# HGRN2 blocks half a period behind the RWKV blocks, and head totals as two fp32r passes over a split operand

## The chip, the cores and the metric

The kernel runs on one core of one Trainium2 chip. The metric is the device time of one execution in microseconds: 2369.66 us, the median of three runs (2367.89 to 2370.66).

## The reference, cut to what matters

Two layers work on a sequence of 2048 tokens with 1024 features. Layer 0 projects its modulated input to nine streams of 512 columns, and mixes them in two ways. The HGRN2 half has 4 heads of 128 columns; the RWKV half has 8 heads of 64 columns. Layer 1 is a gated linear recurrence (RG-LRU). Each layer ends with an output projection, a residual and a layer norm. What is computed in the places that the change touches:

```python
# HGRN2, per head of 128: chunked decayed attention, then
o = o * lax.rsqrt(jnp.mean(o * o, -1, keepdims=True) + RMS_EPS)
# RWKV-7, per head of 64:
kk = heads(k * k_k)
kk = kk * lax.rsqrt(jnp.maximum(jnp.sum(kk * kk, -1, keepdims=True), 1e-24))
y = rwkv7_scan(rh, heads(decay), kh, vh, -kk, kk * icl)
y_var = jnp.mean(jnp.square(y - y_mu), -1, keepdims=True)
y = y + jnp.sum(rh * kh * r_k.astype(f32), -1, keepdims=True) * vh
```

The three totals over a head of 64 (of `kk*kk`, of `rh*kh*r_k`, of the squared centred `y`) are the totals that the change rewrites.

## The kernel before

The tokens go through in two superblocks of 1024 (`sb`), each of two halves of 512 (`b`). For every layer and superblock there are a preparation of the input (`make_h`, `prep_h`), a mixer (`mix0`, `mix1`) and an output stage (`out_proj`). Every large projection is three passes of fp32r matmuls over operands split into a high and a low part (`mm3`, L430 to L433; `split`, L366).

The order of TensorE in `mix0` (L1227 to L1284) is written by hand. `projections()` yields once per step, and one step is two of the eight `k` of a projection, so six matmuls of 128x512. 16 steps are the low-rank projection, then 48 steps per group `g` (three RWKV and three HGRN2 projections of two halves), and 64 steps are the gates. The other work is a list of tasks, each with the step at which it starts; a task goes on until its next `yield n` and comes back `n` steps later. The other engines are ordered by a list scheduler in which earlier written instructions have precedence, and `tc.high_priority(offset=n)` moves an instruction up by `n`.

For a group `g` and a half `b` an RWKV block (`b_steps`, L844) starts at step 40+48g+24b, and the HGRN2 block of the same `g`, `b` (`a_steps`, L630) at 64+48g+24b, which is the step at which the next RWKV block starts. The period is thus 24 steps. With the start of the block as step 0, TensorE does in an RWKV block: `pss` (total for `kk`) at 2, `psc` at 8 and 10, `pbn` and `pv` at 12, `pk` at 14, `pzt` and `pg` at 16, then the 16x16 triangular inverse on VectorE (L969 to L974, 15 pairs of a multiply and a reduce), which goes out to DRAM and comes back as `xd` (L977 to L982) and is transposed to `xn` (L984); `plq` at 22 reads `xn`; `pzq` at 24, four ScalarE copies into `x32` (L1008), the transpose `xm` (L1010, named `xn` in the code), `plx` at 26, `pz` 28, `pwv` 30, `pmq` 32, the eight states one step apart from 34 (`pn`, each followed by L1090 on VectorE), `py` at 42 and `pvr` (total for the variance) at 44. In an HGRN2 block: the decays of levels 5 and 0 at 0, `scores` of these and the decays of levels 1 and 2 at 4, `scores` of these, the decays of 3 and 4 and the exponentials at 8, the last `scores` at 14, `pk` at 16, `pst` at 18, `po` at 20, `pss` at 22. The total in that block (L785, L786) is already two fp32r passes over a split operand.

The three totals of an RWKV block are one fp32 matmul each with the block matrix `bones` (L864, L925, L1112). There are 16 RWKV blocks in the run.

The gates (`gate_steps`, L570) follow from step 208; at step 256 the output weights are fetched (`fetch`, L474) into tiles whose tags are listed in `WO0` (L60), four of which are tags of the HGRN2 block, and `half` (L487) splits them at 264 and 272. Projection results, inputs and gates live in tiles of the pool `up` (L101), 11 of them.

Of the kernel before, what the change touches and what calls it, by code (L numbers as in the profile page):

```python
# [13 lines left out]
F32 = mybir.dt.float32  # L14
F32R = mybir.dt.float32r
BF16 = mybir.dt.bfloat16
U8 = mybir.dt.uint8
AF = mybir.ActivationFunctionType
ALU = mybir.AluOpType
# [4 lines left out]
P = 128  # L24
# [7 lines left out]
INV_STEPS = 6  # L32
# [23 lines left out]
for _n, _w in VEC_FIELDS:  # L56
# [1 line left out]
    _o += _w  # L58
NVEC = _o
WO0 = (  # L60
    (1, "b_kk", 1), (1, "b_m1", 1), (1, "b_ep", 1), (3, "b_bk", 1), (1, "a_b", 1), (1, "a_e", 1), (1, "a_lf", 1),
    (1, "a_kz", 1), (2, "b_zg", 1), (2, "b_bkt", 1), (2, "b_sv", 2),
)

DBG = {}
# [3 lines left out]
def tile_encoder(  # L69
# [19 lines left out]
    nc = tc.nc  # L89
# [8 lines left out]
    cst = ctx.enter_context(tc.tile_pool(name="cst", bufs=1))  # L98
    hp = ctx.enter_context(tc.tile_pool(name="hp", bufs=1))
    wp = ctx.enter_context(tc.tile_pool(name="wp", bufs=4))  # L100
    up = ctx.enter_context(tc.tile_pool(name="up", bufs=11))  # L101
    sp_ = ctx.enter_context(tc.tile_pool(name="sp", bufs=1))
    pool = [None]

# [12 lines left out]
    tp = _Cur()  # L117
# [13 lines left out]
    make_identity(nc, ident)  # L131
    ones = cst.tile([P, 1], F32, name="ones")
    nc.vector.memset(ones, 1.0)
    bones = cst.tile([P, P], F32, name="bones")
    nc.vector.memset(bones, 1.0)
    ones_r = cst.tile([P, P], F32R, name="ones_r")
    nc.vector.tensor_copy(ones_r, bones)
    nc.vector.memset(bones[0:64, 64:128], 0.0)
    nc.vector.memset(bones[64:128, 0:64], 0.0)

    cen = cst.tile([P, P], F32, name="cen")
    nc.vector.scalar_tensor_tensor(out=cen, in0=bones, scalar=-1.0 / 64.0, in1=ident, op0=ALU.mult, op1=ALU.add)
# [6 lines left out]
    def V(name, i):  # L149
        o = VOFF[name] + i  # L150
        return vec[:, o : o + 1]
# [214 lines left out]
    def split(hi, lo, src, eng=None, hi_eng=None):  # L366
        (hi_eng or nc.scalar.copy)(hi, src)  # L367
        return (eng or nc.vector).tensor_tensor(out=lo, in0=src, in1=hi.bitcast(F32), op=ALU.subtract)  # L368
# [434 lines left out]
    xd = cst.tile([P, 8, 32], F32, name="xd")  # L803
    nc.gpsimd.memset(xd, 0.0)

    def rate_steps(p, sb, b, lr, sgi_of):

        sgi = sgi_of[p, b] = tp.tile([P, 2, BLK], F32, name=f"sgi_{p}_{sb}_{b}", tag="sgi")
        w2a2_sb = tp.tile([P, P], F32, name=f"w2a2_{p}_{sb}_{b}", tag="w2a2")
        nc.sync.dma_start(w2a2_sb, w2a2[:, p * P : (p + 1) * P])  # L810
        yield 2
        ls = slice(b * BLK, (b + 1) * BLK)

        pws = [ps.tile([P, BLK], F32, name=f"pw_{p}_{sb}_{i}_{b}", tag="tb", bufs=2) for i in range(2)]
        for i in range(2):
            rows = slice(64 * i, 64 * i + 64)
            nc.tensor.matmul(pws[i], w2a2_sb[rows], lr[rows, ls], start=True, stop=True)
        for i, bias in enumerate(("w0", "a0")):
            last = nc.scalar.activation(sgi[:, i], pws[i], AF.Sigmoid, bias=V(bias, p))
        ln_exp_after(last)  # L820
# [23 lines left out]
    def b_steps(p, sb, b, us, sgi_of):  # L844
# [3 lines left out]
        nm = f"b{p}_{sb}_{b}"  # L848
# [9 lines left out]
        ep = tp.tile([P, 8, 65], F32, name=f"ep_{nm}", tag="b_ep")  # L858
        sq = ep.rearrange("p c t -> p (c t)")[:, 0:BLK]
        nc.scalar.activation(sq, k, AF.Square, scale=V("kk", p))  # L860
        nc.scalar.activation(kkr, k, AF.Identity, scale=V("kk", p))
        yield 2
        pss = ps.tile([P, BLK], F32, name=f"pss_{nm}", tag="tb", bufs=2)
        nc.tensor.matmul(pss, bones, sq, start=True, stop=True)  # L864
        m = t2k("b_m1")
        mx = nc.vector.tensor_scalar_max(m, pss, 1e-24)
        exact_ln(m, m, mx, scale=131072.0)
# [24 lines left out]
        nc.vector.tensor_mul(bk[:, :, 1], v64(icl), v64(em))  # L892

        nc.vector.scalar_tensor_tensor(out=icl, in0=r, scalar=V("rk", p), in1=icl, op0=ALU.mult, op1=ALU.mult)

        sc = tp.tile([P, 2, 8, P], F32, name=f"zb_{nm}", tag="b_sc", bufs=2)
        msk = bmask.rearrange("p (o c) -> p o c", o=1).broadcast_to([P, 4, P])
# [24 lines left out]

        yield 2
        pbn = ps.tile([P, BLK], F32, name=f"pbn_{nm}", tag="tb", bufs=2)
        nc.tensor.matmul(pbn, bones, icl, start=True, stop=True)  # L925

# [37 lines left out]
        nc.gpsimd.memset(xt, 0.0)  # L966
        for q in range(2):
            nc.gpsimd.memset(xt.rearrange("p n i -> p (n i)")[64 * q : 64 * q + 64, q:128:18], 1.0)
        for i in range(1, 16):  # L969
            n = i // 2 + 1  # L970
            pv_ = pr[:, 0 : n * (i + 1)].rearrange("p (n j) -> p n j", j=i + 1)
            av = ai[:, 0 : i + 1, i].rearrange("p (o j) -> p o j", o=1).broadcast_to([P, n, i + 1])
            nc.vector.tensor_mul(pv_, xt[:, 0:n, 0 : i + 1], av)
            nc.vector.tensor_reduce(out=xt[:, 0:n, i], in_=pv_, axis=AX.X, op=ALU.add)  # L974
        xd_dr = dram.tile([8, 8, 8, 2, 16], F32, name=f"xd_{nm}", tag="xd", bufs=2)
        for q in range(2):
            nc.sync.dma_start(xd_dr[:, :, :, q].rearrange("kb c n j -> (kb c) n j"), xt[64 * q : 64 * q + 64])  # L977
# [6 lines left out]
        nc.vector.transpose(xn, xd)  # L984
        x32 = tp.tile([P, 8, 32], F32, name=f"x32_{nm}", tag="b_ai")
        nc.gpsimd.tensor_copy(x32, xd)
        yield INV_STEPS

        plq = ps.tile([P, 8, 16], F32, name=f"plq_{nm}", tag="tb", bufs=2)
        for c in range(8):  # L990
# [16 lines left out]
        for hb in range(4):  # L1007
            nc.scalar.copy(x32[32 * hb : 32 * hb + 16, :, 16:32], pzq[32 * hb : 32 * hb + 16])  # L1008
        xn = tp.tile([P, 8, 32], F32, name=f"xm_{nm}", tag="b_xn")
        nc.vector.transpose(xn, x32)  # L1010
        tt = tt_tiles[tt_count[0] % 2]
        tt_count[0] += 1
        for hb in range(4):
            rs_ = slice(32 * hb, 32 * hb + 32)
            o_ = 32 * (hb % 2)
            nc.gpsimd.tensor_copy(tt[rs_, :, o_ : o_ + 32], x32[rs_])
        yield 2
        plx = ps.tile([P, 8, 32], F32, name=f"plx_{nm}", tag="tb", bufs=2)
        for c in range(8):
            for hd in range(2):  # L1020
# [50 lines left out]


        yield 2
        st = tp.tile([P, 7, 64], F32, name=f"sb_{nm}", tag="b_st")
        pn = ps.tile([P, 8, 64], F32, name=f"pn_{nm}", tag="cg")
        for c in range(8):
            for hd, hs in hds:
# [6 lines left out]
        for c in range(8):  # L1084
            if states[c] is not None:
                for hd, hs in hds:
                    nc.tensor.matmul(
                        pn[hs, c], sc[hs, 0, c, 0:64], states[c][hs], start=False, stop=True, skip_group_check=True
                    )
            nc.vector.tensor_scalar_mul(states[c + 1], pn[:, c], lam[:, c : c + 1])  # L1090
            yield 1
        py = ps.tile([P, 8, 64], F32, name=f"py_{nm}", tag="yb")
        for c in range(8):
# [13 lines left out]
        yp = py.rearrange("p c t -> p (c t)")  # L1107
        sq = zf[:, 0:BLK]
        nc.scalar.activation(sq, yp, AF.Square)
        yield 2  # L1110
        pvr = ps.tile([P, BLK], F32, name=f"pvr_{nm}", tag="cg")
        nc.tensor.matmul(pvr, bones, sq, start=True, stop=True)  # L1112
        rs = zf[:, BLK : 2 * BLK]
        nc.scalar.activation(rs, pvr, AF.Ln, scale=1.0 / 64.0, bias=eps_gn)
        nc.scalar.activation(rs, rs, AF.Exp, scale=-0.5)
# [111 lines left out]
    def mix0(sb, hs, w_first):  # L1227


        lr = tp.tile([P, SBT], F32, name=f"lr{sb}", tag="lr")  # L1230
        sgi_of, tail = {}, []
        plan = out_weights(0, sb, w_evo, lambda: [
            tp.tile([P, n, BLK], F32, name=f"wo0_{sb}_{i}", tag=tag, bufs=bufs)
            for i, (n, tag, bufs) in enumerate(WO0)
        ])
        ub = [[[None, None] for _ in range(3)] for _ in range(4)]
        ua = [[[None, None] for _ in range(3)] for _ in range(4)]

        def projections():
            yield from low_rank(sb, hs, lr, w_first)  # L1240
            for g in range(4):
                for i in range(3):
                    key = f"b{sb}_{i}_{g}"
                    yield from proj_steps(w_ev[16 + 4 * i + g], key, hs, evac_lerp(key, i, g, ub[g][i]))
                for i in (1, 2, 0):
                    ct = 4 * i + g
                    key = f"a{sb}_{ct}"
                    yield from proj_steps(w_ev[ct], key, hs, evac_u(key, (0, ct), 0, ua[g][i]))
            yield from gate_steps(
                0, sb, hs, w_ev, lambda k: 12 + k if k < 4 else 28 + k, (0, 1, 2, 4, 5, 6, 3, 7), tail, plan  # L1250
            )

        tasks = []
        if sb == 0:
            tasks.append((18, late_modulation_steps(0, (4, 5))))
        if sb == NSB - 1:
            tasks.append((18 if NSB > 1 else 36, late_modulation_steps(1, range(6))))
        for g in range(4):
            for b in range(2):
                early = 4 if g == 3 and b else 0  # L1260
                tasks.append((34 + 48 * g + 24 * b - early, rate_steps(g, sb, b, lr, sgi_of)))
                tasks.append((40 + 48 * g + 24 * b - early, (g, b, b_steps, ub)))
                tasks.append((64 + 48 * g + 24 * b, (g, b, a_steps, ua)))

        tasks = [[at, task] for at, task in tasks]
        steps = projections()
        now = 0
        with tc.manual_schedule(engines={nc.tensor.engine}):
            while tasks or steps is not None:
                if steps is not None and next(steps, "end") == "end":  # L1270
                    steps = None
                now += 1
                for entry in list(tasks):
                    if entry[0] > now:
                        continue
                    if isinstance(entry[1], tuple):
                        g, b, make, us = entry[1]
                        entry[1] = make(g, sb, b, us[g], sgi_of) if make is b_steps else make(g, sb, b, us[g])
                    wait = next(entry[1], None)
                    if wait is None:  # L1280
                        tasks.remove(entry)
                    else:
                        entry[0] = now + wait
        return tail, plan  # L1284
# [101 lines left out]

# [13 lines left out]
```

## Time and profile before

| | before |
|---|---|
| time, median of three runs | 2369.66 us |
| the profiled execution's own time | 2367.25 us |
| its span, first to last instruction | 2365.5 us |
| TensorE busy | 2194.7 us (93%) |
| VectorE busy | 1455.6 us (62%) |
| ScalarE busy | 1264.6 us (53%) |
| GpSimd busy | 557.7 us (24%) |
| mean granted TensorE clock | 0.969 |

Busy times overlap between engines. A matmul's duration in the profile includes its way through the array; what a matmul takes from the engine is the distance from its start to the start of the next one. The two mixers of layer 0 lie at about 100 to 753 us and 945 to 1569 us of the span.

### The profile page before, as it was taken

The page shows a single profiled execution, that of the slowest core. Times are in us where ns is not written, and L with a number is a line of the kernel's source. Part 1 is how long each engine was busy: PE and PEld are TensorE (multiplying, and loading weights), DVE is VectorE, ACT ScalarE, POOL GpSimd, SP SyncE. Part 2 cuts the span into 40 slices and gives each one's busy share as a digit, 9 for nine tenths or more (in the row PEclk, how much of TensorE's full clock was granted, in tenths as well). Part 3 has the DMA queues.
Part 4 walks back from the last instruction along what each step waited for, and adds up shares of the span by engine and source line. Part 5 has one row for each costly group of instructions (what it writes and reads, how often), then busy time and mean ns, then how long its engine had stood idle before and what let it go on. Part 6 is the DMA issues. An engine that isn't in the chain of part 4 may idle for free. (4 is left out here: it accounts for less than half of the span.)

```text
span 2365.5 us, 45520 instructions
## 1 busy us (share of the span) xinstructions
PE 2194.7 (93%) x18400; PEld 1727.5 (73%) x18400; DVE 1455.6 (62%) x2697; ACT 1264.6 (53%) x2035; POOL 557.7 (24%) x586
## 2 busy tenths in 40 slices
PE   5989999999999999799999999899999999989998
PEld 4767777777777877577677777678777788767776
DVE  6546666667643678466675666436766556766366
ACT  4344655446666633445565456774467643666541
POOL 3311111212111322112111111112334331353321
PEclk7989999999999999899999999999999999999999
DMA  8210111111332637111111113326311564112652
GB/s 299 92 38 27 40 36 35 44 25 42 97 114 82 223 123 248 35 31 38 33 41 35 44 25 118 112 84 237 130 59 63 169 218 156 63 58 94 200 182 98
DMA packets 185938, 229.82 MB, mean 97 GB/s; under 512 B 65912, under 2 KB 99320, under 8 KB 185728
## 3 DMA queue, kind: packets, MB, share of 16 engines
q1 hardware_dynamic: 185728, 226.92, 30.1%
q8 instruction: 144, 2.36, 0.4%
q14 instruction: 66, 0.54, 0.1%
HBM read 175.46 MB, written 51.39 MB: 96 GB/s over the span
## 5 line engine op out<-in xcount | busy, mean ns | idle before, releaser
L431 PE MATMUL pp_g<-hl_h,wh_g 128*128 128x512 f32 x512 | 212.0, 414 | 4.0 <-ACT go L595 4.0
L433 PE MATMUL pp_g<-hh_h,wl_g 128*128 128x512 f32 x512 | 204.0, 398 | 4.0 <-POOL wl_g L368 4.0
L432 PE MATMUL pp_g<-hh_h,wh_g 128*128 128x512 f32 x512 | 204.4, 399 | 0.0
L368 POOL TENSOR_TENSOR wl_g<-raw_g,wh_g 128x512 fp32r<-128x512 f32 x64 | 97.5, 1528 | 349.9 <-ACT wh_g L367 307.8
L431 PE MATMUL po<-hl_wo,wh_mx 128*128 128x512 f32 x448 | 176.3, 393 | 4.0 <-DVE y L527 4.0
L433 PE MATMUL po<-hh_wo,wl_mx 128*128 128x512 f32 x448 | 175.4, 391 | 0.0
L432 PE MATMUL po<-hh_wo,wh_mx 128*128 128x512 f32 x448 | 174.9, 390 | 0.0
L431 PE MATMUL pp_b<-hl_h,wh_b 128*128 128x512 f32 x384 | 167.8, 437 | 5.1 <-ACT cr_b L838 5.1
L431 PE MATMUL pp_a<-hl_h,wh_a 128*128 128x512 f32 x384 | 168.9, 440 | 0.0
L432 PE MATMUL pp_b<-hh_h,wh_b 128*128 128x512 f32 x384 | 153.5, 400 | 0.0
L432 PE MATMUL pp_a<-hh_h,wh_a 128*128 128x512 f32 x384 | 153.4, 399 | 0.0
L433 PE MATMUL pp_a<-hh_h,wl_a 128*128 128x512 f32 x384 | 153.1, 399 | 0.0
L433 PE MATMUL pp_b<-hh_h,wl_b 128*128 128x512 f32 x384 | 152.7, 398 | 0.0
L368 POOL TENSOR_TENSOR wl_a<-raw_a,wh_a 128x512 fp32r<-128x512 f32 x48 | 66.9, 1402 | 329.0 <-ACT wh_a L367 329.0
L368 POOL TENSOR_TENSOR wl_mx<-raw_mx,wh_mx 128x512 fp32r<-128x512 f32 x64 | 80.8, 1268 | 255.7 <-ACT wh_mx L367 255.7
L368 POOL TENSOR_TENSOR wl_b<-raw_b,wh_b 128x512 fp32r<-128x512 f32 x48 | 67.4, 1409 | 269.1 <-ACT wh_b L367 260.0
L431 PEld LDWEIGHTS pp_g<-hl_h,wh_g 128*128 128x128 f32 x512 | 99.0, 193 | 27.8 <-ACT go L595 4.9
L433 PEld LDWEIGHTS pp_g<-hh_h,wl_g 128*128 128x128 f32 x512 | 99.0, 193 | 27.6 <-POOL wl_g L368 5.7
L587 DVE TENSOR_TENSOR go<-go,oi 128x512 f32<-128x512 f32 x64 | 45.9, 722 | 111.0 <-DMA oi<-o_dr 63.8
L432 PEld LDWEIGHTS pp_g<-hh_h,wh_g 128*128 128x128 f32 x512 | 99.4, 194 | 18.9
L433 PE MATMUL pp_c<-hh_h,wl_c 128*128 128x512 f32 x256 | 101.3, 397 | 11.0 <-POOL wl_c L368 9.6
L431 PE MATMUL pp_c<-hl_h,wh_c 128*128 128x512 f32 x256 | 101.6, 397 | 2.7 <-DVE hl_h L368 2.6
(355 smaller groups left out, 5677.8 us busy)
## 6 DMA issues: line engine op xcount, KB each, us to landing
adw<-in_ada_w_dram SPq DMA_DIRECT2D x96, 256.0 KB
oi<-o_dr SPq DMA_DIRECT2D x64, 256.0 KB
m_dr<-go SPq DMA_DIRECT2D x56, 256.0 KB
raw_b<-in_w_ev_dram SPq DMA_DIRECT2D x48, 256.0 KB
raw_a<-in_w_ev_dram SPq DMA_DIRECT2D x48, 256.0 KB
raw_g<-in_w_ev_dram SPq DMA_DIRECT2D x32, 256.0 KB
wo<-in_w_evo_dram SPq DMA_DIRECT2D x32, 256.0 KB
raw_mx<-m_dr SPq DMA_DIRECT2D x32, 256.0 KB
```

The lines of the kernel that those rows point to most:

```text
L368: return (eng or nc.vector).tensor_tensor(out=lo, in0=src, in1=hi.bitcast(F32), op=ALU.subtract)
L431: nc.tensor.matmul(pt, ah, bl, start=first, stop=False)
L432: nc.tensor.matmul(pt, ah, bh, start=False, stop=False)
L433: nc.tensor.matmul(pt, al, bh, start=False, stop=last)
L587: nc.vector.tensor_mul(go[b], go[b], oi[b])
```

## The change

It has these parts.

1. The head totals of an RWKV block become `head_sums`: two fp32r matmuls with `bones_r`, one over the high and one over the low part. For `pss` and `pvr` the high part is a second `Square` on ScalarE written as fp32r, and the low part is a subtract on VectorE; for `pbn`, `split` makes both (a ScalarE copy and a VectorE subtract). These parts lie in tiles of existing tags (`b_m1`, `b_bk`, `b_kk`, `b_wt`, `b_st`).
2. The HGRN2 blocks start 12 steps later, at 76+48g+24b.
3. Inside an RWKV block, the six steps between `pg` and `plq` are written as 1, 1 and 4, with the inverse begun after the first and cut after `i == 9`; the transpose `xm` and the eight state multiplies get `high_priority(offset=300)`; and `plx` comes 4 steps after `pzq` instead of 2, so all that follows comes 2 steps later.
4. `up` has 15 tiles instead of 11. `WO0` uses tags of the RWKV block alone. `bones` moves to the start phase, and the scratch for dynamic DMA is set to 1024.

```diff
+    (1, "b_kk", 1), (1, "b_m1", 1), (1, "b_ep", 1), (3, "b_bk", 1), (2, "b_zg", 1), (2, "b_bkt", 1),
+    (2, "b_sv", 2), (2, "b_sv", 2), (1, "b_bv", 2), (1, "b_bv", 2),
...
-    up = ctx.enter_context(tc.tile_pool(name="up", bufs=11))
+    up = ctx.enter_context(tc.tile_pool(name="up", bufs=15))
...
+    def head_sums(out, hi, lo):
+        nc.tensor.matmul(out, bones_r, hi, start=True, stop=False)
+        nc.tensor.matmul(out, bones_r, lo, start=False, stop=True)
...
         nc.scalar.activation(sq, k, AF.Square, scale=V("kk", p))
+        hi = t2k("b_m1", dt=F32R)
+        nc.scalar.activation(hi, k, AF.Square, scale=V("kk", p))
+        lo = t2k("b_bk", dt=F32R)
+        nc.vector.tensor_tensor(out=lo, in0=sq, in1=hi.bitcast(F32), op=ALU.subtract)
...
-        nc.tensor.matmul(pss, bones, sq, start=True, stop=True)
+        head_sums(pss, hi, lo)
...
+        bn = t2k("b_kk", dt=F32R), t2k("b_m1", dt=F32R)
+        split(*bn, icl)
...
-        nc.tensor.matmul(pbn, bones, icl, start=True, stop=True)
+        head_sums(pbn, *bn)
...
+        yield 1
         for i in range(1, 16):
...
+            if i == 9:
+                yield 1
...
-        yield INV_STEPS
+        yield INV_STEPS - 2
...
-        nc.vector.transpose(xn, x32)
+        with tc.high_priority(offset=300):
+            nc.vector.transpose(xn, x32)
...
-        yield 2
+        yield 4
         plx = ps.tile([P, 8, 32], F32, name=f"plx_{nm}", tag="tb", bufs=2)
...
-            nc.vector.tensor_scalar_mul(states[c + 1], pn[:, c], lam[:, c : c + 1])
+            with tc.high_priority(offset=300):
+                nc.vector.tensor_scalar_mul(states[c + 1], pn[:, c], lam[:, c : c + 1])
...
         nc.scalar.activation(sq, yp, AF.Square)
+        hi = t2k("b_wt", dt=F32R)
+        nc.scalar.activation(hi, yp, AF.Square)
+        lo = t2k("b_st", dt=F32R)
+        nc.vector.tensor_tensor(out=lo, in0=sq, in1=hi.bitcast(F32), op=ALU.subtract)
...
-        nc.tensor.matmul(pvr, bones, sq, start=True, stop=True)
+        head_sums(pvr, hi, lo)
...
-                tasks.append((64 + 48 * g + 24 * b, (g, b, a_steps, ua)))
+                tasks.append((76 + 48 * g + 24 * b, (g, b, a_steps, ua)))
```

## Rows read from the trace of the kernel before

**Rows 1.** Three stretches: length, busy PE, PEld, DVE, ACT, POOL; clock; DMA share; GB/s

```profile
100.00:753.00 653.00, 607.79 (x7049) 467.56 (x7048) 380.74 (x876) 357.70 (x632) 108.36 (x141) 0.96 0.18 50
945.00:1569.00 624.00, 577.43 (x6960) 444.81 (x6961) 377.54 (x879) 342.60 (x608) 102.37 (x135) 0.96 0.18 51
320.00:335.00 15.00, 11.11 (x154) 7.98 (x141) 9.09 (x12) 10.46 (x19) 6.46 (x8) 0.77 0.15 54
```

**Rows 2.** Waits of TensorE over the span: total us, times, longest

```profile
PE plx_b L1023 <- DVE xm_b L1010: 29.1, 14, 3.9
PE psc_b L905 <- DVE bk_b L892: 12.8, 2, 8.4
PE plq_b L994 <- DVE xn_b L984: 11.9, 2, 6.4
PE sc_a L679 <- DVE w_a L667: 11.9, 8, 3.2
PE psc_b L905 <- DVE zb_b L912: 7.4, 12, 0.8
PE pst_a L750 <- ACT a_w_a L745: 6.6, 2, 3.3
```

**Rows 3.** Timeline of TensorE around one total: start, duration, engine, line

```profile
240.30 1.02 PE L1112 MATMUL pvr_b<-zb_b,bones 128*128 128x512 f32 x2
241.16 0.61 PE L772 MATMUL po_a<-st,a_lf_a 128*128 128x128 f32 x4
```

**Rows 4.** The same around the HGRN2 total in two fp32r passes

```profile
460.57 0.39 PE L785 MATMUL pss_a<-a_kz_a,ones_r 128*128 128x512 f32 x1
460.80 0.40 PE L786 MATMUL pss_a<-a_b_a,ones_r 128*128 128x512 f32 x1
```

**Rows 5.** Timeline of ScalarE and TensorE: one square for pss, and that pss

```profile
415.19 0.72 ACT L860 ACTIVATE ep_b<-u_b,vec 128x512 f32<-128x512 f32 x1
...
473.30 2.08 PE L864 MATMUL pss_b<-ep_b,bones 128*128 128x512 f32 x2
```

**Rows 6.** Timeline of ScalarE: the square ahead of pvr

```profile
236.64 0.60 ACT L1109 ACTIVATE zb_b<-py_b 128x512 f32<-128x512 f32 x1 [4.19 <-PE py_b L1101]
```

**Rows 7.** Timeline of ScalarE and VectorE: high and low part of an HGRN2 total

```profile
388.27 0.59 ACT L780 ACTIVATE a_kz_a<-po_a 128x512 fp32r<-128x512 f32 x1
...
390.90 0.68 DVE L782 TENSOR_TENSOR a_b_a<-a_e_a,a_kz_a 128x512 fp32r<-128x512 f32 x1
```

**Rows 8.** Durations of one line: ns minimum, median, maximum, for two lines

```profile
L894 DVE SCALAR_TENSOR_TENSOR sgi<-u_b,vec,sgi x16: 721/745/1785, 136.7 to 1435.5; 128x512 f32<-128x512 f32 x16
...
L782 DVE TENSOR_TENSOR a_b_a<-a_e_a,a_kz_a x16: 681/684/693, 244.6 to 1567.8; 128x512 fp32r<-128x512 f32 x16
```

**Rows 9.** Timeline of GpSimd beside a long L894, and that L894

```profile
414.21 1.54 POOL L368 TENSOR_TENSOR wl_a<-raw_a,wh_a 128x512 fp32r<-128x512 f32 x1 [10.29 <-ACT wh_a L367]
...
414.51 1.78 DVE L894 SCALAR_TENSOR_TENSOR sgi<-u_b,vec,sgi 128x512 f32<-128x512 f32 x1
```

**Rows 10.** Timeline of all engines from pzq to plx of one block

```profile
395.83 0.64 PE L1004 MATMUL pzq_b<-xd,lq_b 32*16 32x16 f32 x58
...
397.19 1.08 ACT L1008 COPY x_b<-pzq_b 16x128 f32<-16x128 f32 x4
...
397.69 2.13 DVE L645 TENSOR_TENSOR_SCAN a_b_a<-smask,a_lf_a 128x512 f32<-128x512 bf16 x1
...
400.51 0.43 DVE L1010 STREAM_TRANSPOSE xm_b<-x_b 128x256 f32<-128x256 f32 x1
...
401.00 0.69 PE L1023 MATMUL plx_b<-xm_b,zb_b 32*32 32x32 f32 x32 [1.58 <-DVE xm_b L1010]
```

**Rows 11.** Timeline of all engines from the inverse to plq of one block

```profile
448.22 0.29 DVE L974 TENSOR_REDUCE xt_b<-pr_b 128x8 f32<-128x128 f32 x1
...
457.62 0.45 DVE L984 STREAM_TRANSPOSE xn_b<-xd 128x256 f32<-128x256 f32 x1 [5.17 <-DMA xd<-xd_b]
...
461.52 0.65 PE L994 MATMUL plq_b<-xn_b,zb_b 32*32 32x16 f32 x56 [0.33 <-ACT sgi L819]
```

**Rows 12.** Busy time by stretch: the end of the first mixer (columns as in rows 1)

```profile
676.00:706.00 30.00, 24.37 (x283) 18.99 (x281) 11.11 (x18) 25.45 (x42) 5.06 (x6) 0.83 0.35 106
755.00:785.00 30.00, 30.00 (x134) 24.82 (x133) 14.10 (x20) 29.65 (x40) 8.28 (x7) 1.00 0.40 125
```

More of the change, by code (lines that the diff above doesn't have):

```diff
@@ L60 @@
 WO0 = (
-    (1, "b_kk", 1), (1, "b_m1", 1), (1, "b_ep", 1), (3, "b_bk", 1), (1, "a_b", 1), (1, "a_e", 1), (1, "a_lf", 1),
-    (1, "a_kz", 1), (2, "b_zg", 1), (2, "b_bkt", 1), (2, "b_sv", 2),
+    (1, "b_kk", 1), (1, "b_m1", 1), (1, "b_ep", 1), (3, "b_bk", 1), (2, "b_zg", 1), (2, "b_bkt", 1),
+    (2, "b_sv", 2), (2, "b_sv", 2), (1, "b_bv", 2), (1, "b_bv", 2),
 )
@@ L133, in tile_encoder @@
     nc.vector.memset(ones, 1.0)
-    bones = cst.tile([P, P], F32, name="bones")
+    bones = tp.tile([P, P], F32, name="bones")
     nc.vector.memset(bones, 1.0)
@@ L139, in tile_encoder @@
     nc.vector.memset(bones[64:128, 0:64], 0.0)
+    bones_r = cst.tile([P, P], F32R, name="bones_r")
+    nc.vector.tensor_copy(bones_r, bones)
     cen = cst.tile([P, P], F32, name="cen")
@@ L1073, in b_steps @@
         yield 2
-        st = tp.tile([P, 7, 64], F32, name=f"sb_{nm}", tag="b_st")
+        st = tp.tile([P, 8, 64], F32, name=f"sb_{nm}", tag="b_st")
         pn = ps.tile([P, 8, 64], F32, name=f"pn_{nm}", tag="cg")
@@ L1388 @@
     arrays = lay_out({k: np.asarray(v) for k, v in inputs.items()})
-    nc = bacc.Bacc("TRN2", target_bir_lowering=False, num_devices=1)
+    nc = bacc.Bacc("TRN2", target_bir_lowering=False, num_devices=1, dynamic_dma_scratch_size=1024)
     aps = [
```

## The prediction

> **What bounds the kernel now.** I read the page's busy times, then the stretches, then TensorE's waits, then the timeline around the three places that wait most. TensorE is busy 607.8 of 653 us and 577.4 of 624 us in the two mixers that the change touches [rows 1]. The reader is to see that this engine is the bound, that about 92 us of the mixers it stands idle, and that its granted clock there is 0.96 on average: 4% of 1277 us, or 51 us, is the most that the lower of its two levels (1.2 in place of 2.4 GHz) can have taken. The order of TensorE is fixed, so a late operand stops everything behind it. The waits name VectorE first: `plx` for the transpose `xm` (29.1 us, 14 of 16 blocks), then `psc` for `bk` and `plq` for `xn` (12.8 and 11.9 us, two each, and these are the first RWKV block of a superblock, where little other work lies between), then the `scores` of HGRN2 and the masks of `psc` (11.9 and 7.4 us), and `pst` for ScalarE (6.6 us, at the end of a mixer) [rows 2]. VectorE itself is busy only 58 to 61% there [rows 1]: it is late by its order, not by its amount. The rest of the run (output stages, layer 1) is left alone but for the larger pool.
>
> **The change part by part.** All is summed against the profiled execution, 2367.25 us (span 2365.5, 1.75 around it); it lies 2.4 us under the median of the runs.
>
> *The totals.* One fp32 total holds TensorE 0.86 us, from 240.30 to the next start at 241.16 [rows 3]. One fp32r pass of the same shape holds it 0.23 us (460.57 to 460.80) [rows 4], so two cost 0.46 and 0.40 us is saved. Three totals in 16 blocks are 48, or 19.2 us. This is on the path wherever TensorE doesn't wait directly behind; I take 17. Both ends: 0, and 19.
>
> What it adds is 48 operations on ScalarE and 48 subtracts on VectorE, at the price of the HGRN2 block's own (0.59 and 0.68 us) [rows 7]: 28 and 33 us, on engines busy 55 and 60% [rows 1]. Do they make TensorE wait? For `pss`, no: its square is made at 415.2 and read at 473.3 [rows 5], 57 us ahead, and the low part needs only the tile of the former block's `bk`, which that block reads last at its step 14, ten steps before. `pbn`'s parts are made before `psc`, four steps ahead. `pvr` is the tight one: its square ends at 237.24, 3.06 us before the matmul [rows 3, 6]. The high part takes 0.59 of that; the low part came 2.7 us after the high one in an HGRN2 total (388.86 to 391.58) where VectorE had other work first [rows 7]. In the new order the step of `pvr` meets the exponentials and last decays of the HGRN2 block, so VectorE will have other work. That gives 0 to 1 us in each of 16 blocks; I take 3 us in all.
>
> A row speaks against counting these subtracts at 0.68 us. L894, which also reads two operands from SBUF, takes 0.745 us at the median and 1.785 at most [rows 8], and the long one lies over a GpSimd subtract of 1.54 us [rows 9]; L782, the operation that is copied here, has 0.681 to 0.693 in all 16 [rows 8]. I count by L782, the nearest row. The Trainium skill, "SBUF — State Buffer", section "Who interferes with whom", says that a VectorE instruction with two SBUF inputs contends with a GpSimd instruction that reads SBUF, and that one of the two then waits out the other; by that rule every added subtract is exposed, and the sum would be some 5 us longer (1.1 us for about a third of 16 `pvr`). The trace agrees for L894 and doesn't for L782.
>
> *`plx`.* In the block shown, `pzq` ends at 396.47, the ScalarE copies at 398.27, and VectorE is then in a scan that lasts to 399.82 and in other work, so `xm` starts 2.2 us after its operand; TensorE has waited 1.58 us when `plx` starts [rows 10]. The change takes this from both sides: precedence for `xm`, and two more steps, at least 12 matmuls of 0.23 us, 2.7 us. The longest wait is 3.9 us [rows 2], and precedence removes up to two of these, so I let all 29 us go. Around one such wait the clock is 0.77 over 15 us [rows 1], 3.4 us; the two longest are of this kind and most others cost less, so I take 10 us for the clock. Together 39; I put 1 us back for what remains: 38. Both ends: 10 (the copies themselves late), 43.
>
> *Half a period.* Before, the front of an HGRN2 block (scan, six of the decays' operations, masks) lies on the front of the next RWKV block, up to its step 8, where `psc` needs `bk` and its masks. Afterwards the front lies on steps 12 to 20, and steps 0 to 8 meet the lighter second half. Of the 19.3 us of `scores` and mask waits [rows 2] I take off 9; both ends are all of them gone and as much again. The HGRN2 work is missing for 12 steps more beside the second RWKV block of a superblock, whose chain from `pss` to `psc` has then less to hide behind; 3 us for both, between 0 and the 8.4 us of the first block's worst [rows 2].
>
> What now stands under the HGRN2 front is the inverse. In the block shown it ends at 448.51, its way through DRAM lasts until `xn` starts at 457.62, and `plq` starts at 461.52: 3.5 us to spare after `xn` [rows 11], and the two new cuts let HGRN2 operations go ahead of it. Cost below: 0. Above: see the third rival. I take 6 us, less than half a microsecond in each of 14 blocks, since the inverse needs only its operand from DRAM and VectorE has 40% free.
>
> *The end of a mixer.* The last HGRN2 block now ends 12 steps later, among the gates and the split of the output weights. ScalarE is busy 29.65 of 30 us there, and TensorE 30.00 of 30; in the stretch from 676 us, where that block's front now lies, they have 25.45 and 24.37, with a clock of 0.83 [rows 12]. So work moves from a place that stalls to one that is full. The block's six ScalarE operations after `scores` are 3.6 us at 0.59 [rows 7], twice. I take 5 us of new waits net of what the first place gains; both ends 13 less and 25 more. The read of `o_dr` for the last gate is queued on SP behind the later store; the loads of the output stage are given precedence and wait for the first half only, so I count nothing.
>
> *Pool and scratch.* 15 tiles carry the three more that 12 steps fill (two per 8 steps); without them the evacuations would stop. Earlier gate loads in layer 1: 1 us, between 0 and 8.
>
> Sum: −17 +3 −38 −9 +3 +6 +5 −1 = −48. Profiled 2319, median 2322; own range 2302 to 2342.
>
> **The rivals.**
>
> *First: the waits move instead of going.* The totals pay (17), `plx` no longer waits (38), but 36 us of new waits come where HGRN2 and RWKV now meet: `plq`, `pvr`, the HGRN2 `scores`. For it: VectorE's operations number the same plus 48, and every wait in rows 2 is one of order. Against: 40% of VectorE is free. 2369.7 − 17 − 38 + 36 = 2351, from 2342 to 2367.
>
> *Second: better than that.* Also the waits at the end of the mixer and all of the `scores` go: 19 for 17, 43 for 38, 19 for 9, and none of the 17 us that I added: −82, about 2288. Against: the full ScalarE [rows 12].
>
> *Third, slower: the inverse is late in every block.* A serial chain of 30 small operations meets the HGRN2 front: the scan of 2.13 us [rows 10], three operations of the kind of L782 and twelve of the decays at no more than its 0.68 [rows 8] are 12.3 us. If two thirds of that goes ahead, `xn` comes 8 us later, `plq` waits 4.6 us, and with the clock as at `plx` (39 us lost for 29.1 us waited, a factor 1.34) 14 blocks lose 86 us in place of my 6: 2322 + 80 = 2402. It turns the sign when `plq` waits 2.9 us per block (54 / 14 / 1.34), so with `xn` 6.3 us later than now. Against: the inverse can run as soon as its operand lands.
>
> *That the passes don't pay* would need an fp32r pass of 0.43 us; rows 4 has 0.23 for the same shape, so I give it no chance of its own; half a saving lies in the first rival.
>
> **How the numbers follow.** Forecast 0.55, first rival 0.26, second 0.08, third 0.11. The range of 2296 to 2365 leaves out half of the second rival, the third, and the end of the first. What this measurement can't tell from no change is 0.2%, 2364.9 to 2374.4: 0.05, the end of the first rival. Slower 0.11, faster 0.84.
>
> **What would show it.** In the changed trace: `head_sums` in pairs 0.23 us apart, and the next start 0.46 us after the first; no wait of `plx` on `xm`; `plq` waiting on `xn` only in the first block of a superblock; `pvr`'s second pass waiting under 1 us; the clock in both mixers near 0.98 in place of 0.96. Wrong would be: waits of `plq` in all blocks (third rival), a mixer that isn't shorter by 20 us each, or an end of the mixer, from the last `pmq` to the first `po`, longer by more than 10 us.

## The result and the profile after

The changed kernel takes 2383.5 us (median of 4 runs, 2377.9 to 2384.5) against 2368.8 us for the kernel before (median of 4): a ratio of 1.0054, with an interval of 1.0040 to 1.0067. It is slower by 0.5%; the prediction was 2322 us. The profiled execution took 2377.9 us, with a span of 2376.2 us and a mean clock of 0.961.

The two mixers, busy time by stretch (columns as in rows 1):

```profile
100.00:753.00 653.00, 603.64 (x7062) 473.99 (x7061) 395.15 (x896) 380.63 (x663) 105.24 (x143) 0.96 0.18 53
945.00:1569.00 624.00, 567.39 (x6894) 444.50 (x6893) 385.75 (x888) 355.26 (x624) 97.28 (x135) 0.95 0.18 52
```

In the same stretches TensorE is busy 4 and 10 us less than in [rows 1], and the clock is no better: the engine stands more. Its waits over the span (total us, times, longest), and under them the one row of the kernel before that the first is to be held against:

```profile
PE pn_b L1104 <- DVE sb_b L1108: 34.2, 14, 4.3
PE pzq_b L1020 <- ACT lq_b L1014: 17.6, 8, 2.6
PE plq_b L1010 <- DVE xn_b L1000: 14.4, 2, 7.5
...
PE psc_b L918 <- DVE bk_b L903: 11.1, 2, 7.3
```

```profile
PE pn_b L1087 <- DVE sb_b L1090: 1.8, 2, 0.9
```

Beside [rows 2] the reader is to see three things. The waits that the change was costed to remove are gone: `plx` on `xm` (29.1 us), the HGRN2 `scores` and the masks of `psc`. Those of the first RWKV block of a superblock stayed (`plq`, `psc`). New are 34.2 us of `pn`, which waits for the state multiply L1108 in 12 of the 16 blocks (1.8 us before), and 17.6 us of `pzq` (none before). Summed over both mixers, up to the first `po`, TensorE stands 110 us (92 before), and 123 us lie at the lower clock level, 1.2 in place of 2.4 GHz (102 before).

The place of a `pn` wait. VectorE's timeline (start, duration, line, output and inputs), then TensorE's and GpSimd's at the same time:

```profile
428.62 1.29 DVE L987 TENSOR_TENSOR pr_b<-xt_b,ai_b 128x2 f32<-128x2 f32 x1 [2.55 <-POOL ai_b L978]
429.95 0.15 DVE L988 TENSOR_REDUCE xt_b<-pr_b 128x1 f32<-128x2 f32 x1
...
430.62 0.69 DVE L871 TENSOR_TENSOR b_bk_b<-ep_b,b_m_b 128x512 fp32r<-128x512 f32 x1
...
431.84 0.95 DVE L987 TENSOR_TENSOR pr_b<-xt_b,ai_b 128x18 f32<-128x18 f32 x1
...
433.04 0.21 DVE L987 TENSOR_TENSOR pr_b<-xt_b,ai_b 128x28 f32<-128x28 f32 x1
433.16 0.28 DVE L1108 TENSOR_SCALAR sb_b<-pn_b,lam_b 128x64 f32<-128x64 f32 x1
```

```profile
428.20 0.33 PE L1104 MATMUL pn_b<-sb_b,zb_b 64*64 64x64 f32 x4
433.49 0.33 PE L1104 MATMUL pn_b<-sb_b,zb_b 64*64 64x64 f32 x4 [3.37 <-DVE sb_b L1108]
```

```profile
428.46 0.13 POOL L978 MEMSET ai_b<- 128x16 f32 x1 [21.75 <-DMA ai_b<-ad_b]
428.60 1.30 POOL L370 TENSOR_TENSOR wl_b<-raw_b,wh_b 128x512 fp32r<-128x512 f32 x1
```

The state's matmul ends at 428.5, but its multiply stands in VectorE's queue behind the first operations of the *next* block's inverse. These had stood for 2.55 us because their operand was just landing from DRAM, and then take 4.5 us; the multiply starts at 433.16 and TensorE has waited 3.37 us. Among what stands ahead of it is the low part of a `pss` (L871), which the passes added. Behind it the clock is 0.72 over 6 us (434 to 440). In 12 of the 16 blocks three of the eight state multiplies of a block stand ahead of the next block's inverse, and these are the 12 in which `pn` waits; in the kernel before it was five.

The place of a `pzq` wait, ScalarE's timeline, then TensorE's:

```profile
376.82 0.69 ACT L826 ACTIVATE sgi<-pw,vec 128x512 f32<-128x512 f32 x1
378.45 1.28 ACT L668 ACT_TABLE_LOAD   x1 [0.94 <-DVE w_a L667]
...
381.43 1.28 ACT L826 ACT_TABLE_LOAD   x1
382.73 0.69 ACT L826 ACTIVATE sgi<-pw,vec 128x512 f32<-128x512 f32 x1
383.44 1.28 ACT L353 ACT_TABLE_LOAD   x1
384.73 0.69 ACT L1136 ACTIVATE zb_b<-pvr_b,eps_gn 128x512 f32<-128x512 f32 x1
385.32 0.26 ACT L1014 COPY lq_b<-plq_b 128x128 f32<-128x128 f32 x1
```

```profile
385.63 0.54 PE L1020 MATMUL pzq_b<-xd,lq_b 32*16 32x16 f32 x48 [2.03 <-ACT lq_b L1014]
```

A table load (`ACT_TABLE_LOAD`, 1.28 us) stands in these rows wherever ScalarE goes from one kind of function to another: sigmoid (L826), exponential (L668), the logarithm behind `pvr` (L1136). The two sigmoids of a block are torn apart by the exponentials of the HGRN2 block, which costs two more of them, and `lq` comes behind all of them: `plq` had started at 379.91, `lq` starts at 385.32 and `pzq` at 385.63, after 2.03 us of waiting.

The totals are as forecast:

```profile
379.36 0.39 PE L810 MATMUL pvr_b<-b_wt_b,bones_r 128*128 128x512 f32 x1
379.58 0.40 PE L811 MATMUL pvr_b<-b_st_b,bones_r 128*128 128x512 f32 x1
379.91 0.73 PE L1010 MATMUL plq_b<-xn_b,zb_b 32*32 32x16 f32 x64
```

The second pass starts 0.22 us after the first, and the next matmul 0.55 us after the first, against 0.86 in [rows 3]. All sixteen `pvr` together waited 0.2 us for their parts.

### The profile page after: what moved, and what is told of

It is laid out like the page before. It is cut to its first block, busy times and chain, and to the rows that moved or that the text cites. A ratio compares the mean times of both kernels' runs of the same rounds, so it can differ in the third digit from the quotient of the medians.

```text
span 2376.2 us, 45600 instructions
## 1 busy us (share of the span) xinstructions
PE 2185.7 (92%) x18400; PEld 1738.7 (73%) x18400; DVE 1493.2 (63%) x2746; ACT 1297.0 (55%) x2085; POOL 547.5 (23%) x586
## 5 line engine op out<-in xcount | busy, mean ns | idle before, releaser
L433 PE MATMUL pp_b<-hl_h,wh_b 128*128 128x512 f32 x384 | 162.6, 423 | 7.9 <-ACT cr_b L845 7.9
L589 DVE TENSOR_TENSOR go<-go,oi 128x512 f32<-128x512 f32 x64 | 47.4, 741 | 109.1 <-DMA oi<-o_dr 61.3
L987 DVE TENSOR_TENSOR pr_b<-xt_b,ai_b 128x2 f32<-128x2 f32 (+14 forms) x240 | 83.1, 346 | 47.7 <-POOL ai_b L978 38.3
```

The costliest lines, as they stand in the source:

```text
L433: nc.tensor.matmul(pt, ah, bl, start=first, stop=False)
L589: nc.vector.tensor_mul(go[b], go[b], oi[b])
```

## The experiments

All ratios are to the kernel before, timed beside each group of runs, with 95% intervals.

**1. The parts alone.** `shift_only` is the kernel before with the HGRN2 blocks at 76, the pool of 15 and the new `WO0`; `passes_only` has the two-pass totals alone; `intra_only` the inner edits of the RWKV block alone (inverse in three parts, both precedences, `plx` four steps after `pzq`); `no_shift` is the changed kernel with the line below undone. The first three keep the scratch size of part 4.

```diff
-                tasks.append((76 + 48 * g + 24 * b, (g, b, a_steps, ua)))
+                tasks.append((64 + 48 * g + 24 * b, (g, b, a_steps, ua)))
```

> The kernel before with the HGRN2 blocks 12 steps later (and the pool of 15 and the weight tags that this needs), totals and RWKV steps as before. Theory A: the eight states of one RWKV block now meet the inverse of the next; `pn` waits on `sb` 25 to 40 us, `pzq` on `lq` is there too, and the time is 2385 to 2405 us, slower than the whole change, because the passes' 19 us are missing. Theory B: no such waits without the added operations; 2340 to 2365 us.

> The kernel before with the three totals in two fp32r passes and nothing else. Theory A (the passes pay what they should, and the shift of the HGRN2 blocks makes the new waits): 48 x 0.40 us saved less a few us of waits, so 2350 to 2356 us, `pn` on `sb` under 3 us in all as before, `plx` on `xm` near 29 us as before. Theory B (the 96 added operations on ScalarE and VectorE are what makes `lq` and `sb` late): 2365 to 2380 us, with waits of `pzq` on `lq` and of `pn` on `sb` here already.

> The kernel before with only the steps and precedences inside the RWKV block changed (inverse cut in two, `xm` and states with precedence, `plx` two steps later). Theory A: `plx` on `xm` goes (29 us waited and about 10 us of clock), the states don't meet the inverse, so 2325 to 2345 us. Theory C (cutting the inverse and giving the states precedence is itself what delays `xn` and `sb`): `pn` on `sb` over 20 us or `plq` on `xn` in most blocks, 2365 to 2395 us.

> The changed kernel with the HGRN2 blocks back at 64 instead of 76. Theory A: all that was forecast but the shift: passes and `plx`, 2310 to 2330 us, waits of `pn` on `sb` under 8 us, of `pzq` on `lq` under 5 us. Theories B and C: the waits stay, 2365 to 2390 us.

| kernel | us (runs) | ratio |
|---|---|---|
| `shift_only` | 2344.4 (4) | 0.9900 [0.9866, 0.9933] |
| `passes_only` | 2358.6 (10) | 0.9958 [0.9941, 0.9975] |
| `intra_only` | 2426.0 (4) | 1.0258 [1.0223, 1.0292] |
| `no_shift` | 2429.6 (4) | 1.0260 [1.0231, 1.0289] |

The shift and the passes each gain; the inner edits cost 57 us by themselves, which no expectation allowed for (`intra_only` and `no_shift` lie above every range given; `passes_only` falls between its two). What `plx` waited for goes by the shift alone, nearly all of it. Waits of TensorE in `shift_only`, then in `intra_only`:

```profile
PE pn_b L1094 <- DVE sb_b L1097: 11.8, 9, 3.9
...
PE plx_b L1030 <- DVE dec_a L740: 7.7, 2, 4.0
```

```profile
PE sc_a L681 <- DVE w_a L669: 47.4, 18, 3.3
PE pn_b L1098 <- DVE sb_b L1102: 36.0, 14, 3.6
```

The waits of `plx` on `xm` are down to 2.7 us in `shift_only`, while `intra_only` has the waits of `pn` of the changed kernel. Its longest wait, though, is that of the HGRN2 `scores` for their masks, 47.4 us after 11.9 [rows 2] (59.3 in `no_shift`): without the shift as much of the new waiting lies there as at `pn`.

**2. Which inner edit.** `no_intra` has the passes and the shift without any inner edit. The others undo one edit in the changed kernel: `after_plx2` the two steps (the diff below), `after_noprio` the precedence of the state multiplies, `after_nocut` the cut of the inverse.

```diff
-        yield 4
+        yield 2
         plx = ps.tile([P, 8, 32], F32, name=f"plx_{nm}", tag="tb", bufs=2)
```

> Passes and shift, with the steps and precedences inside the RWKV block as before. The three runs so far: passes alone -10 us, shift alone -24, the block's inner changes alone +57. If the parts add, 2368.7 - 10 - 24 = 2335 us, `pn` on `sb` some 12 us as with the shift alone. Rival: the passes' additions meet the shift's full ScalarE and the two don't add, 2345 to 2360 us.

> The changed kernel with `plx` again 2 steps after `pzq`, so the states, `py` and `pvr` two steps earlier. Theory P (the two steps put states and `pvr` onto the next block's inverse and sigmoids): 2335 to 2350 us and `pn` on `sb` under 15 us, though `plx` may wait on `xm` again a little. Theory Q (precedence of the states) and R (the cut inverse): stays at 2375 to 2390 us.

> The changed kernel without precedence for the state multiplies. Theory Q (VectorE, in order, is made to stop at a state multiply whose `pn` isn't there yet, and HGRN2's operations queue behind it): 2340 to 2355 us. Theories P and R: within 8 us of 2383, `pn` on `sb` 34 us or more.

> The changed kernel with the inverse written in one piece right after `pg`, six steps ahead of `plq`. Theory R (the cuts move the inverse so that it meets the states): 2340 to 2360 us with `pn` on `sb` under 15 us. Theories P and Q: within 8 us of 2383.

| kernel | us (runs) | ratio |
|---|---|---|
| `no_intra` | 2318.4 (4) | 0.9789 [0.9764, 0.9814] |
| `after_plx2` | 2318.1 (2) | 0.9792 [0.9758, 0.9825] |
| `after_noprio` | 2381.1 (6) | 1.0056 [1.0035, 1.0076] |
| `after_nocut` | 2380.7 (4) | 1.0070 [1.0042, 1.0099] |

One digit, two steps between `pzq` and `plx`, costs 65 us. The precedence of the states and the cut of the inverse, each taken back in the changed kernel, move the time by 3 us at most, and `no_intra`, which takes back the precedence of `xm` too, equals `after_plx2`. Both lie under their expected ranges. Waits in `after_plx2`:

```profile
PE plq_b L1010 <- DVE xn_b L1000: 19.7, 9, 7.1
...
PE pn_b L1104 <- DVE sb_b L1108: 10.3, 7, 3.0
...
PE plx_b L1040 <- DVE xm_b L1027: 9.7, 4, 3.0
```

Against the changed kernel `pn` is down by 24 us and `pzq` is gone, while `plx` waits 9.7 and `plq` 5 us more. TensorE stands 66 us in the mixers in place of 110, and 85 us in place of 123 lie at the lower clock level, which is half the speed: 44 + 38/2 = 63 us, about the 65.

**3. Why two steps cost that.** Three ways to take the collisions away with `plx` left where the change put it. `after_inv` adds an order edge: the first operation of an inverse may stand in VectorE's queue only behind the latest state multiply that is written when the inverse is. In the trace six of the eight then stand ahead of it.

```diff
+            if i == 1 and last_state[0] is not None:
+                with tc.issue_after(last_state[0].ins):
+                    nc.vector.tensor_mul(pv_, xt[:, 0:n, 0 : i + 1], av)
...
+                last_state[0] = nc.vector.tensor_scalar_mul(states[c + 1], pn[:, c], lam[:, c : c + 1])
```

`after_rate32` moves the sigmoids two steps ahead, `after_inv_rate32` does both, and `after_retime` keeps `plx` and brings what follows back to its former steps. First the edit of `after_rate32`, then that of `after_retime`:

```diff
-                tasks.append((34 + 48 * g + 24 * b - early, rate_steps(g, sb, b, lr, sgi_of)))
+                tasks.append((32 + 48 * g + 24 * b - early, rate_steps(g, sb, b, lr, sgi_of)))
```

```diff
-        yield 2
+        yield 1
         for c4 in range(2):
             cs4 = slice(4 * c4, 4 * c4 + 4)
             pw = ps.tile([P, 4, 2, 64], F32, name=f"pwv_{nm}_{c4}", tag=("yb", "cg")[c4])
...
-        yield 2
+        yield 1
         for c4 in range(2):
             cs4 = slice(4 * c4, 4 * c4 + 4)
             pm = ps.tile([P, 4, 2, 64], F32, name=f"pmq_{nm}_{c4}", tag=("yb", "cg")[c4])
```

> The changed kernel with one order edge: the first operation of an inverse (L987) may stand in VectorE's queue only behind the latest state multiply (L1108) of the block before it. Theory S (the 65 us are the sum of separate collisions that the two steps set up, each removable where it stands): the 14 waits of pn for the state multiply (34.2 us in the changed kernel, 10.3 with plx two steps earlier) fall to about 10, with the half clock behind them some 30 us of the run: 2350, from 2340 to 2362. Theory C (the later chain itself holds the next block, wherever it is late): the inverse becomes late by what the states gain, plq waits for xn in most blocks (over 30 us) and the time stays within 2370 to 2400.

> The changed kernel with the rate steps (matmuls L824, sigmoids L826) two steps earlier, so that ScalarE does not go from sigmoid to exponentials and back to sigmoid around pvr and plq. Theory S: pzq no longer waits for lq (17.6 us in 8 blocks), table loads fall from 173 to near 161 (12 of 1.28 us on ScalarE), the run by 17.6 x 1.34 = 24 us: 2360, from 2348 to 2370. Theory C: pzq waits go, but pn, plq or plx wait instead, and the time stays within 2372 to 2390.

> The changed kernel with plx still four steps after pzq, and the two later distances pz to pwv and pwv to pmq cut from 2 steps to 1, so that pmq, the eight states, py and pvr stand at the steps that they have with plx two steps earlier (2318 us). Theory S: what hurts is where states and pvr stand against the next block's inverse and sigmoids, not where plx stands; pn waits about 10 us, pzq waits gone, table loads near 159: 2325, from 2316 to 2340, plus what pwv and pmq now wait for their shorter distances (tt, wt: under 1 us in each of 16 blocks). Theory C (plx itself later is the cost): 2365 to 2385.

> Both the order edge of the inverse and the rate steps two steps earlier, in the changed kernel with plx still four steps after pzq. Theory S: both waits gone, 2328, from 2318 to 2345; what is left above 2318 are the waits of pzt and pz at the end of a mixer (10.1 and 5.8 us). Theory C: 2365 to 2385.

| kernel | us (runs) | ratio |
|---|---|---|
| `after_inv` | 2397.8 (2) | 1.0129 [1.0072, 1.0186] |
| `after_rate32` | 2368.1 (8) | 1.0000 [0.9978, 1.0023] |
| `after_retime` | 2313.1 (2) | 0.9771 [0.9713, 0.9829] |
| `after_inv_rate32` | 2414.3 (2) | 1.0199 [1.0139, 1.0258] |

`after_retime` decides it: with `plx` four steps after `pzq` the time is 2313 us (3 us under the range), so the price is that of `pmq`, the states, `py` and `pvr` standing two steps later. Theory S was right in that and wrong in a point that `after_inv` shows. Waits of `after_inv`, of `after_inv_rate32`, of `after_rate32` and of `after_retime`:

```profile
PE plq_b L1015 <- DVE xn_b L1005: 82.2, 15, 9.6
```

```profile
PE plq_b L1015 <- DVE xn_b L1005: 110.6, 16, 9.8
```

```profile
PE pn_b L1104 <- DVE sb_b L1108: 37.3, 14, 4.7
...
PE pzq_b L1020 <- ACT lq_b L1014: 9.7, 8, 3.1
```

```profile
PE plq_b L1010 <- DVE xn_b L1000: 18.8, 7, 7.4
...
PE pn_b L1104 <- DVE sb_b L1108: 9.9, 7, 2.8
```

With the order edge `pn` hardly waits any more, and `plq` waits 82.2 us in 15 blocks: the inverse starts 44 us after its block's `pss` in place of 36, and its result is late by more than the states gained, as theory C had it. Of the two orders tried at these steps, each makes one of the chains lose; an order that mixes them more finely was not tried. With the sigmoids moved as well (`after_inv_rate32`) `plq` waits 110.6 us, and the time, 2414 us, lies above both theories. Moving the sigmoids saves 15 us (24 were expected): half the `pzq` wait stays, the table loads fall from 173 to 161, and the `pn` waits are untouched. That is the one measure of ScalarE's part in the 65 us.

The place of the `pn` wait in `after_retime`, VectorE and TensorE:

```profile
417.62 0.16 DVE L987 TENSOR_TENSOR pr_b<-xt_b,ai_b 128x2 f32<-128x2 f32 x1 [1.13 <-POOL ep_b L883]
...
418.69 0.27 DVE L1108 TENSOR_SCALAR sb_b<-pn_b,lam_b 128x64 f32<-128x64 f32 x1
...
421.07 0.28 DVE L1108 TENSOR_SCALAR sb_b<-pn_b,lam_b 128x64 f32<-128x64 f32 x1
```

```profile
416.84 0.33 PE L1104 MATMUL pn_b<-sb_b,zb_b 64*64 64x64 f32 x4
419.02 0.33 PE L1104 MATMUL pn_b<-sb_b,zb_b 64*64 64x64 f32 x4 [0.25 <-DVE sb_b L1108]
```

Five states are through when the inverse begins, the sixth follows 1.1 us after the start of it, and TensorE waits 0.25 in place of 3.37 us.

**4. How far the place goes.** `plx3` has `plx` three steps after `pzq`; `plx2_retime` has it two steps after and the shorter distances of `after_retime` besides; `intra_retime` is `intra_only` with these distances; `retime_again` times `after_retime` once more.

> The changed kernel with plx three steps after pzq in place of four: the states stand one step earlier, and four state multiplies of a block stand ahead of the next block's inverse in VectorE's queue (three in the changed kernel, five with plx at two). Theory S (the place of the states against the inverse sets the time): between the two, 2335 to 2368, with pn waiting for the state multiply some 20 us. Theory T (the number of ScalarE table loads, 169 here, sets it): 2368 to 2380.

> The changed kernel with plx two steps after pzq and pwv and pmq one step closer: states, py and pvr stand two steps earlier than in the 2318 us kernel, and seven of eight state multiplies stand ahead of the inverse. Theory S with more room: pn waits under 5 us and plq for xn under 20, 2300 to 2318. Against it: the states of a block then meet more of the HGRN2 front of other steps, and sigmoids and logarithms alternate again (169 table loads): 2318 to 2345.

> The kernel before with the inner changes alone (inverse in three parts, both precedences, plx four steps after pzq) and the two later distances cut by one step each, so that five state multiplies stand ahead of the inverse as in the kernel before (2 in the run with the inner changes alone, 2426 us). Theory S: the 57 us that the inner changes cost go, and the wait of plx for xm goes too: 2335 to 2365. Theory C (the cost of the inner changes is elsewhere, in the precedences or the cut): over 2390.

> The changed kernel with plx four steps after pzq and pwv and pmq one step closer, timed again: 2313 as before, 2309 to 2318.

| kernel | states ahead of the inverse | us (runs) | ratio |
|---|---|---|---|
| changed kernel | 3 | 2383.5 (4) | 1.0054 [1.0040, 1.0067] |
| `plx3` | 4 | 2353.7 (2) | 0.9934 [0.9914, 0.9954] |
| `retime_again` | 5 | 2313.2 (4) | 0.9760 [0.9744, 0.9777] |
| `plx2_retime` | 7 | 2383.2 (2) | 1.0058 [1.0035, 1.0081] |
| `intra_retime` | 5 | 2367.9 (8) | 0.9998 [0.9982, 1.0013] |

From three to five each step is worth 30 to 40 us, but the count of states is not all that changes with a step. Waits of `plx3`, of `plx2_retime` and of `intra_retime`:

```profile
PE pn_b L1104 <- DVE sb_b L1108: 27.9, 18, 3.5
...
PE pzq_b L1020 <- ACT lq_b L1014: 5.9, 4, 1.6
```

```profile
PE plq_b L1010 <- DVE xn_b L1000: 40.9, 14, 7.2
PE pwv_b L1066 <- ACT tt L1054: 27.8, 16, 2.5
```

```profile
PE pz_b L1045 <- ACT lx_b L1038: 21.0, 14, 3.3
PE sc_a L681 <- DVE w_a L669: 13.8, 13, 2.8
```

The first of the steps, from the changed kernel to `plx3`, takes 11.7 us from `pzq` and 6.3 from `pn`, the second 18 from `pn` and the other 5.9 from `pzq`: the two collisions go together, and no run takes away that of the states alone. In `plx2_retime` `pn` waits only 5.5 us, but `pwv` waits for ScalarE's `tt` and `plq` for `xn`, and 2383 us lies above both expected ranges: more room is no better, and not by the same mechanism. Why `plq` is late there stays open; the inverse starts 39 us after `pss` (36 in `after_plx2`). `intra_retime` gives back the 57 us of `intra_only`, as expected, but nothing of the 29.1 us at `plx` [rows 2]: without the shift the wait moves on to `pz`, which stands two steps behind, and the time misses its range by 3 us. `after_retime` is the fastest version measured: 2313.2 us, 2.4% under the kernel before. `after_plx2` and `no_intra` are 5 us slower, which the intervals don't tell apart.

## Why the prediction was wrong, step by step

**The step that failed is `plx`, −38.** I costed the two more steps as a distance for `plx` alone, "at least 12 matmuls of 0.23 us", and no term of the sum asked what the eight states, `py` and `pvr`, which come two steps later with it, meet there (for `pvr` I counted only its own two parts). That place cost 65 us: the state multiplies fell behind the next block's inverse in VectorE's fixed order (`pn` waits 34.2 us, 10.3 without the two steps), and ScalarE's sigmoids, exponentials and the logarithm of `pvr` fell into each other (17.6 us of `pzq`, none without), each with its share of the clock. How the 65 us divide between the two is not shown, but for the 15 us that `after_rate32` gets back. The gain at `plx` was real in the trace, but it belonged for the most part to the shift: `shift_only` has 2.7 us of waits on `xm` left, `no_intra` 9.5, and precedence and steps add nothing that can be measured (2318.4 without the inner edits, 2318.1 with all but the two steps). Alone, `intra_only`, they lose 57. By the prediction's own sign of being wrong the mixers were to be shorter by 20 us each: the first `po` comes at 776 us after 778, the second at 1603 after 1594.

**Totals, −17 and +3.** Alone −10 us, four short of my −14. The saving per total is there: from the first pass to the next start 0.55 us at `pvr` (0.86 before) and 0.66 at `pbn` (1.06 before), medians of 16. At `pss` this distance hides it (0.57 after 0.56), because the next matmul before started early and took longer; from the third matmul ahead of `pss` to the third start behind it, it is 1.42 us in `passes_only` after 1.82. Every `pvr` has its parts in time. What is short is not in one place: in `passes_only` the HGRN2 `scores` wait 22.3 us in place of 11.9, `plx` 15.4 in place of 29.1, TensorE's idle time in the mixers is 4 us more, and 109 us in place of 102 lie at the lower clock level. Counting the added subtracts at 0.68 us held in the changed kernel, where the two of them at L871 and L1131 have means of 0.73 and 0.67; in `after_retime` L871 has 1.13.

**Half a period, −9 and +3, inverse +6, end of the mixer +5, pool −1.** Together I gave these +4; measured alone, `shift_only`, they are −24, with the waits of `plx` that I had booked elsewhere among what goes. The end of the mixer, from the last `pmq` to the first `po`, is 75.2 and 75.8 us in `shift_only` after 72.4 and 72.2, so the +5 for both was about right; in the changed kernel, where `pmq` itself stands two steps later, it is 70.5. `plq` waits only in the first blocks in the changed kernel, as forecast. Passes and shift together gain 50 us, 16 more than the two alone. What I summed as −48 is what the change gains without the two steps, but by other terms than mine, the shift in place of `plx`, so that the sum comes so near (−50) is luck.

**The rivals.** The first, waits that move, names the kind of what happened, in a wrong place and at half its size. The third has the right mechanism, the inverse against other work in VectorE's order, with the wrong partner and loser: I set it against the HGRN2 front and let `plq` wait, while it met the state multiplies and `pn` waited. `after_inv` turned this into the third rival itself: 82.2 us of `plq`.

**Clock.** I expected 0.98; the changed kernel has 0.96 and 0.95 in the stretches above, and both mixers of `after_retime` 0.97. The clock followed the waits: 102 us at the lower level with 92 us of standing before, 123 with 110 in the changed kernel, 85 with 66 in `after_plx2`.

## What to carry to other kernels

A step put in between moves everything behind it, so list each operation that comes later with it and look up what it meets there on the in-order queues of the other engines. Where two serial chains share an engine, count how many links of the one stand ahead of the other: if swapping them only moves the wait, as `after_inv` did here, try distance before precedence, and not more of it than the wait asks for (`plx2_retime`). When several edits seem to earn one gain, run the sum with each left out; here the edit that was to earn most cost more than all it stood beside.

## What the runs showed of the hardware

The same VectorE operation takes more or less time from one placement to the next. Three groups of the changed kernel (busy, mean ns of one, idle before), then the same of `after_retime`:

```profile
L905 DVE SCALAR_TENSOR_TENSOR sgi<-u_b,vec,sgi 128x512 f32<-128x512 f32 x16 | 22.4, 1397 | 0.2
L987 DVE TENSOR_TENSOR pr_b<-xt_b,ai_b 128x2 f32<-128x2 f32 x16 | 13.7, 857 | 41.0 <-POOL ai_b L978 38.3 <-POOL ep_b L883 2.7
L871 DVE TENSOR_TENSOR b_bk_b<-ep_b,b_m_b 128x512 fp32r<-128x512 f32 x16 | 11.6, 727 | 6.1 <-PE pk_b L957 4.3 <-ACT b_m_b L869 1.8
```

```profile
L905 DVE SCALAR_TENSOR_TENSOR sgi<-u_b,vec,sgi 128x512 f32<-128x512 f32 x16 | 12.0, 747 | 0.2
L987 DVE TENSOR_TENSOR pr_b<-xt_b,ai_b 128x2 f32<-128x2 f32 x16 | 3.7, 229 | 18.4 <-POOL ep_b L883 10.5 <-POOL ai_b L978 7.8
L871 DVE TENSOR_TENSOR b_bk_b<-ep_b,b_m_b 128x512 fp32r<-128x512 f32 x16 | 18.1, 1129 | 14.3 <-PE pk_b L957 12.6 <-ACT b_m_b L869 1.8
```

A multiply of two columns takes 1.29 us at 428.62 and ends as GpSimd's subtract (428.60, 1.30 us) ends, while the reduce behind it takes its usual 0.15. Ten of the 16 such multiplies of the changed kernel take 1.26 to 1.29 us, each up to within 0.02 us of the end of a GpSimd subtract, and the other six 0.16 to 0.17; in `after_retime` it is one of 16. The Trainium skill, "SBUF — State Buffer", section "Who interferes with whom", says that a VectorE instruction with two SBUF inputs contends with a GpSimd instruction that reads SBUF. Here the trace agrees. Such contention moves with the steps: L905 has a mean of 1.40 us in the changed kernel and 0.75 in `after_retime`, so a duration from the profile of before is safe only while its neighbours stay. Whether it is a part of the 65 us was not tried apart. All operations of the 16 inverses together take 132.5 us on VectorE in the changed kernel and 121.5 in `after_plx2`, so inside them it is 11 us at most.
